# The retention branch's SiLU gate formed where its projection leaves PSUM, and multiplied onto each retention block

## The chip, the cores and the metric

One core of one Trainium2 chip runs the whole program. The metric is the device time of one execution in microseconds. A few names are used throughout: PE is the tensor engine (matmuls, with weight loads listed as PEld), DVE the vector engine, ACT the scalar engine, POOL the engine called GpSimd, and SP the engine whose queue issues every DMA of this kernel. SBUF is the working memory of 128 partitions; PSUM holds what PE writes, in eight banks of 128 x 512 float32 values. Each engine works its own queue in order and waits on semaphores for the others.

## The reference, cut to what matters

One layer is applied to 2048 frames of a new stream and to 64 frames of a running one. A combined projection of 1024 to 6144 columns feeds a differential attention (branch A), a multi-scale retention (branch B), a SiLU gate for each branch (za, zb) and two sigmoid merge gates.

```python
h = rmsnorm(x, norm_g) @ w_in
qa, ka, va, za, qb, kb, vb, zb, ga, gb = jnp.split(h, _split_points(), axis=-1)
...
oa = diff_attention(...)          # 4 heads, 128-d values
ob = retention(...)               # 4 heads, blocks with a carried state
...
oa = (rmsnorm(oa, subln_g) * (1.0 - lam_init)).reshape(B, T, W_A) * jax.nn.silu(za)
ob = rmsnorm(ob).reshape(B, T, W_B) * jax.nn.silu(zb)
m = ga * (oa @ w_oa) + gb * (ob @ w_ob)
return x + m @ w_out
```

The change concerns the line for `ob`: where silu(zb) is formed, and where it is multiplied.

## The kernel before

Matrices are split into a high and a low part (`hi`, `lo`, suffixes `h` and `l`), and three float32r matmuls stand for one product. The frames are worked in two halves of 1024; the 64 sample frames go with the first.

The instruction order is not written out. Each piece of work is a Python generator; a loop runs them by priority over modelled clocks (`self.pe`, `self.act`, `self.dve`, `self.pool`, moved by `P`, `A`, `V`, `G`, with `ld` and `st` for DMAs). A generator yields a modelled time, or a condition, at which it may go on. The order in which generators emit is the order in each engine's queue, and the hardware then runs these fixed queues with its real durations. `take` and `give` count the buffers of a tag (`BUFS`): `mm` 2, `s` 2, `at` 2, `pv` 1 and `tp` 1 are PSUM banks; `ev` 3 and `tlo` 2 are eviction tiles; `row` 10 are the large working rows; `oz` 11, `og` 16 and `ob` 8 serve the output stage.

Three streams run beside one another. `w_stream` (lowest priority) walks through the projection's column blocks of 256: keys, queries and values of the attention first, then vb, qb, kb, then a mark "ret", then za, zb, ga, gb. For a gate it calls `transposed`: `mm_group` (L533, matmuls at L554) fills an `mm` bank with 128 output channels of 512, 320 or 256 frames, and `fin_t` (L853) evicts it: one DVE multiply by the row's RMS factor (L865) into an `ev` tile, the bank given back, and a store to a DRAM scratch tensor (`zaT`, `zbT`, `gaT`, `gbT`). `z_stream` does attention and retention: `qk_block` writes scores to `s` banks (L1052, L1053), DVE evicts them with the distance bias (L1061), softmax runs on ACT and DVE, and `at_pv` transposes and multiplies by the values. The retention blocks (`ret_block`, L1463, 17 of them) follow after the half's attention, and in half 1 partly between heads; each ends with a transpose (L1563), an ACT copy to `res` and four stores to `obT`.

When `z_stream` is done, `out_prep` (L1634) loads, for each group of 264 frames and each branch, four tiles `on` (from `oaT` or `obT`) and four tiles `z`; `og_fin` (L1661) applies SiLU to `z` on ACT (L1664), multiplies on POOL (L1667) and splits the product (ACT cast to `ogh` L1677, DVE subtraction to `ogl` L1680). `out_stream` consumes them in `m_tile` (L1722 to L1724, eight tiles a group, branch A into an `mm` bank, branch B into an `s` bank). The products have buffers for three sets of four, so the set for a group's branch can be cast only when the set three before has had its last matmul. Beside it `gates` loads the merge gates (`gt`, tanh at L1698), `m_fin` combines on DVE (L1742) and POOL (L1746), and `b_prep` prepares the last projection's weights (`wst`, casts to `bh` and `bht` at L1815). The last projection (L1934) closes the program.

Of the kernel before, what the change touches and what calls it, by code (L numbers as in the profile page):

```python
# [11 lines left out]
AF = mybir.ActivationFunctionType  # L12
# [14 lines left out]
GW = 264  # L27
# [9 lines left out]
LAT = 250.0  # L37
# [22 lines left out]
class Hybrid:  # L60
# [771 lines left out]

        return fin

    def transposed(self, half, dst, d0, scale=None, grouped=True, final=False):
        us = []
        groups = [(0, 0, 512), (1, 0, 256), (1, 256, 320)] if half == 0 else [(0, 0, 512), (1, 0, 512)]
        for ct in range(2):
            for k, (seg, col, n) in enumerate(groups):
                yield from self.take("mm")  # L840
                ps = self.psum("mm")[:, :n]
                last = ct == 1 and k == len(groups) - 1
                yield from self.mm_group(ps, n, us, slice(128 * ct, 128 * ct + 128),
                                         (seg, slice(col, col + n)), True, last)
                t0 = 1024 * half + 512 * seg + col
                self.live["t"] += 1
                self.spawn(self.fin_t(ps, n, dst[d0 + ct], t0, scale, grouped, self.pe + LAT), 0, "w")
# [5 lines left out]
    def fin_t(self, ps, n, dst, t0, scale, grouped, t):  # L853
        nc = self.nc
        c0 = t0 % 1024
        last = 8 if n % 128 else (c0 + n) // 128 - 1
        yield lambda: self.tb[last] is not None
        yield from self.take("ev")
        ev = self.sb(self.ep, [128, 512], "ev")[:, :n]
        t = max(t, self.tb[last])  # L860
        if t > self.pe:
            yield t
        rsb = self.rsb[:, c0:c0 + n]
        if scale is None:
            nc.vector.tensor_mul(ev, ps, rsb)  # L865
# [597 lines left out]
    def ret_block(self, k, t0, r, first):  # L1463
        nc = self.nc
        z0 = 0 if r == 128 else 4
# [7 lines left out]
        qt, kt, qx = v3(qk, 0), v3(qk, 1), v3(vx, 1)  # L1473
# [3 lines left out]
        t = self.ld(vb, self.vbN[t0:t0 + r, :], 1 << 18)  # L1477
# [18 lines left out]
        ts = self.V(4 * r, t)  # L1496
# [18 lines left out]
        ru = self.row("rru")  # L1515
# [3 lines left out]
        for h in range(4):  # L1519
            oh = op[:, 128 * h:128 * h + 128]  # L1520
            nc.tensor.matmul(oh, sm[:, h, :], vb[:, 128 * h:128 * h + 128], start=True, stop=first)  # L1521
            to = self.P(512)
            if not first:
                nc.tensor.matmul(oh, qx[:, h, :], state[:, 128 * h:128 * h + 128], start=False, stop=True)
                to = self.P(512)
        if tu > self.pe:
            yield tu
        new = self.sb(self.tp_, [128, 512], "state")
        if first:
            nc.vector.tensor_copy(new, up)  # L1530
            t = self.V(512, tu)
        else:
            for h in range(4):
# [3 lines left out]
                t = self.V(128, tu)  # L1537
# [16 lines left out]
        t = self.V(80)  # L1554
# [23 lines left out]
        self.give("row", self.pe, 2)  # L1578
        self.give("row", t)

    def ret_some(self, b0, n):
# [52 lines left out]
    def out_prep(self):  # L1634
        pa = self.z3p
        self.wo = [[([[self.sb(self.zq, [128, 512], "wa", "woq", F32R) for n in "hl"],
                      [pa.tile([128, 512], F32R, tag=f"wo{n}{br}{kt}", name=f"wo{n}{br}{kt}") for n in "hl"]], {})
                    for kt in range(4)] for br in range(2)]
        for br in range(2):
            yield from self.load_wo(br, 0)  # L1640
        for g in range(8):
            gsl = slice(GW * g, GW * g + GW)
            for br, (oT, zT) in enumerate(((self.oaT, self.zaT), (self.obT, self.zbT))):
                for kt in range(4):
                    yield from self.take("oz", 2)
                    on = self.sb(pa, [128, GW], "oz", "on")
                    z = self.sb(pa, [128, GW], "oz", "z")
                    self.ld(z, zT[kt][:, gsl], 1 << 17)
                    t = self.ld(on, oT[kt][:, gsl], 1 << 17)
                    og = []  # L1650
                    self.ogs.append(og)
                    self.spawn(self.og_fin(on, z, t, og, (2 * g + br) % 3 == 2), 1)
                    yield self.pe
            if g == 0:
                self.spawn(self.gates(), 0)
                for q in range(1, 4):
                    for br in range(2):
                        yield from self.load_wo(br, q)
                yield lambda: self.b_left < 13

    def og_fin(self, on, z, t, og, third):  # L1661
        nc = self.nc
        yield t
        nc.scalar.activation(z, z, AF.Silu)  # L1664
        t = self.A(GW, self.pe)
        yield t
        nc.gpsimd.tensor_mul(on, on, z)  # L1667
        t = self.G(GW, t)
        self.give("oz", t)
# [7 lines left out]
        nc.scalar.copy(h, on)  # L1677
        t = self.A(GW, t)
        yield t
        nc.vector.tensor_sub(l, on, h.bitcast(F32))  # L1680
        t = self.V(GW + 80, t)
        self.give("oz", t)
        og.append((h, l, t))
# [388 lines left out]
    def w_stream(self):  # L2072
# [18 lines left out]
                seq.append((base + 256 * g, lambda half, dst=dst, g=g, sc=sc:  # L2091
                            self.transposed(half, dst, 2 * g, sc, False)))
        seq.append((None, "ret"))
        for base, dst, n in ((za, self.zaT, 2), (zb, self.zbT, 2), (ga, self.gaT, 4), (gb, self.gbT, 4)):
            for g in range(n):
                fin = base == gb and g == n - 1
                seq.append((base + 256 * g, lambda half, dst=dst, g=g, fin=fin:
                            self.transposed(half, dst, 2 * g, final=fin)))
# [76 lines left out]
    def run(self):  # L2175
# [21 lines left out]
        for k in ("ac", "u", "xt", "ob"):  # L2197
            self.res[k].free = []
        self.q_end = self.smx = None
        self.y_at, self.yr = -1, []  # L2200
        self.yq = [{} for _ in range(8)]
        ET = mybir.EngineType
# [93 lines left out]
```

## Time and profile before

| | |
|---|---|
| time, three runs | 1944.99, 1946.57 (median), 1947.22 us |
| the profiled execution | 1945.82 us, span 1944.0 us, mean granted PE clock 0.998 |
| instructions in the span | 33842 |
| DMA | 301 MB in 371904 packets, 52.6% of 16 engines' span |

Below are the page's rows by slices. Each digit is the busy share of one fortieth of the span (48.6 us) in tenths; PEclk is the clock that PE was granted.

```profile
PE   9999999999999999999999999999999999999999
DVE  6753777646666336648856757845773376545643
ACT  7443766544434235535765646544563445653321
POOL 4310112112122121211121111112113356543422
```

PE is nearly full in every slice. DVE varies most: it is high where attention and projection run beside one another, and low at 600 to 720 us and around 1520 us. The output stage (from about 1575 us) is the one place where POOL and ACT rise together. The first gate block is evicted at 385 us, and its places in both halves lie in stretches in which DVE also serves attention. In rows of the views, "idle before" is the time for which an engine sat waiting, with what ended the wait.

### The profile page before, as it was taken

To read this page: it belongs to the slowest core of one execution; us is meant where nothing else is said; L and a number is where in the kernel's file an instruction comes from. 1 tells how busy PE (TensorE), PEld (TensorE's weight loads), DVE (VectorE), ACT (ScalarE), POOL (GpSimd) and SP (SyncE) were. 2 spreads that over 40 slices of the span, in tenths; PEclk is the share of its full clock that TensorE was granted. 3 is DMA by queue.
4 is the path that set the end of the run, shared out by engine and by line. 5 is a ranking of instruction groups with operands and counts; after the bars stand their busy time and mean duration, and the time that the engine had idled before them with its cause. 6 is when DMAs were issued, how large, how long until landed. Compare 5 with 4: busy or idle time off the path is not lost.

```text
span 1944.0 us, 33842 instructions
## 1 busy us (share of the span) xinstructions
PE 1927.5 (99%) x11984; PEld 1731.2 (89%) x11984; DVE 1166.6 (60%) x2798; ACT 964.9 (50%) x2072; POOL 490.1 (25%) x429
## 2 busy tenths in 40 slices
PE   9999999999999999999999999999999999999999
PEld 8779999999988899999998888888888889998887
DVE  6753777646666336648856757845773376545643
ACT  7443766544434235535765646544563445653321
POOL 4310112112122121211121111112113356543422
PEclk9999999999999999999999999999999999999999
DMA  7747454335566655654344253363133678866651
GB/s 235 240 151 199 143 143 132 106 102 156 163 192 187 166 148 168 202 183 141 112 120 128 76 146 96 99 185 116 63 99 108 190 229 259 264 196 189 190 151 65
DMA packets 372074, 303.32 MB, mean 156 GB/s; under 512 B 77440, under 2 KB 334720, under 8 KB 371904
## 3 DMA queue, kind: packets, MB, share of 16 engines
q1 hardware_dynamic: 371904, 301.16, 52.6%
q8 instruction: 94, 1.54, 0.4%
q14 instruction: 76, 0.62, 0.1%
HBM read 195.87 MB, written 100.14 MB: 152 GB/s over the span
## 4 chain that ended last, share of the span: by engine, by line
PE 88%; DVE 5%; DMA 3%; POOL 1%; issue 1%; ACT 1%; SPq 1%; DVEq 0%; POOLq 0%; ACTq 0%
PE mm L554 51%; PE mm L1934 4%; PE s L1052 3%; PE s L1053 3%; PE at L1160 3%; PE at L1934 2%; PE pv L1139 2%; PE pv L1140 2%; PE pv L1138 2%; PE s L1934 1%; PE s L1723 1%; PE s L1724 1%; PE pv L1521 1%; PE mm L1723 1%; PE s L1722 1%
## 5 line engine op out<-in xcount | busy, mean ns | idle before, releaser
L514 POOL TENSOR_TENSOR wl<-ws,wh 128x512 fp32r<-128x512 f32 x191 | 261.4, 1380 | 896.2 <-ACT wh L504 544.9
L554 PE MATMUL mm<-xh,wh 128*128 128x512 f32 (+2 forms) x1280 | 460.7, 360 | 0.0
L554 PE MATMUL mm<-xh,wl 128*128 128x512 f32 (+2 forms) x1280 | 452.7, 354 | 0.0
L554 PE MATMUL mm<-xl,wh 128*128 128x512 f32 (+2 forms) x1280 | 451.9, 353 | 0.0
L554 PEld LDWEIGHTS mm<-xh,wl 128*128 128x128 f32 x1280 | 241.0, 188 | 31.7
L554 PEld LDWEIGHTS mm<-xh,wh 128*128 128x128 f32 x1280 | 241.4, 189 | 29.1 <-issue 0.2
L554 PEld LDWEIGHTS mm<-xl,wh 128*128 128x128 f32 x1280 | 241.6, 189 | 27.8
L554 PE MATMUL mm<-wh,xh 128*128 128x256 f32 (+1 forms) x768 | 236.7, 308 | 0.0
L554 PE MATMUL mm<-wh,xl 128*128 128x256 f32 (+1 forms) x768 | 231.3, 301 | 0.0
L554 PE MATMUL mm<-wl,xh 128*128 128x256 f32 (+1 forms) x768 | 231.0, 301 | 0.0
L1175 DVE TENSOR_TENSOR atl<-at,ath 128x512 fp32r<-128x512 f32 (+1 forms) x144 | 93.7, 659 | 136.2 <-ACT ath L1173 136.1
L504 ACT CAST wh<-ws 128x512 fp32r<-128x512 f32 x192 | 117.0, 617 | 112.6 <-PE mm L554 90.3
L1091 ACT ACTIVATE row<-row,a_mx 128x1024 f32<-128x1024 f32 (+7 forms) x160 | 153.7, 962 | 24.5 <-DVE a_mx L1071 24.3
L554 PEld LDWEIGHTS mm<-wh,xh 128*128 128x128 f32 x768 | 146.3, 190 | 7.1 <-issue 0.5
L554 PEld LDWEIGHTS mm<-wl,xh 128*128 128x128 f32 x768 | 146.4, 191 | 6.7 <-issue 0.5
L554 PEld LDWEIGHTS mm<-wh,xl 128*128 128x128 f32 x768 | 146.3, 190 | 5.5
L865 DVE TENSOR_TENSOR ev<-mm,rsb 128x512 f32<-128x512 f32 x140 | 83.0, 593 | 112.8 <-PE mm L554 112.4
L1173 ACT CAST ath<-at 128x512 fp32r<-128x512 f32 (+1 forms) x144 | 78.7, 563 | 141.5 <-PE at L1160 138.4
L1061 DVE CUSTOM_DVE_ANT_0 row<-s,dfar 128x512 f32<-128x512 f32 (+2 forms) x192 | 118.2, 630 | 46.4 <-PE s L1053 45.9
L1052 PE MATMUL s<-K,q 128*128 128x512 f32 (+3 forms) x320 | 118.4, 374 | 0.7 <-DVE a_acc L1061 0.7
L1053 PE MATMUL s<-K,q 128*128 128x512 f32 (+3 forms) x320 | 115.2, 362 | 0.0
L1110 ACT ACTIVATE row<-row,a_w 128x1024 f32<-128x1024 f32 (+4 forms) x96 | 85.1, 898 | 34.4 <-DVE a_w L1105 31.2
(342 smaller groups left out, 4193.5 us busy)
## 6 DMA issues: line engine op xcount, KB each, us to landing
ws<-in_w_in_dram SPq DMA_DIRECT2D x192, 256.0 KB, 3.1
q<-qT SPq DMA_DIRECT2D x128, 128.0 KB, 3.0
V<-vN SPq DMA_DIRECT2D x24, 512.0 KB, 5.4
K<-kT SPq DMA_DIRECT2D x48, 256.0 KB, 4.3
a<-mT SPq DMA_DIRECT2D x34, 256.0 KB, 4.1
gt<-gaT SPq DMA_DIRECT2D x64, 132.0 KB, 3.2
gt<-gbT SPq DMA_DIRECT2D x64, 132.0 KB, 3.1
mT<-gt SPq DMA_DIRECT2D x64, 132.0 KB, 3.0
```

What stands on the lines that cost most here:

```text
L504: self.nc.scalar.copy(h, st)
L514: self.nc.gpsimd.tensor_sub(l, st, h.bitcast(F32))
L554: nc.tensor.matmul(ps, p, q, start=c == 0 and i == 0, stop=c == KC - 1 and i == 2)
L865: nc.vector.tensor_mul(ev, ps, rsb)
L1052: nc.tensor.matmul(ps, q1s, kk, start=True, stop=False)
L1053: nc.tensor.matmul(ps, q2s, kk, start=False, stop=True)
L1061: nc.vector.tensor_tensor_reduce(out=units[k0 // 1024][:, k0 % 1024:k0 % 1024 + n], in0=ps, in1=tab, scale=-SLOPES[h], scalar=3.0e38, op0= ...
L1091: nc.scalar.activation(u, u, AF.Exp, bias=mx, scale=-1.0, accum_out=lp[:, k:k + 1])
L1110: nc.scalar.activation(u1, u1, AF.Identity, scale=w[:, 1:2])
L1173: nc.scalar.copy(ah[:, :w], at[:, :w])
L1175: nc.vector.tensor_sub(al[:, :w], at[:, :w], ah[:, :w].bitcast(F32))
L1934: nc.tensor.matmul(q[b], u, v, start=fresh and c == 0 and m == 0, stop=c == 3 and m == 2, skip_group_check=True)
```

## The change

Four things are changed.

1. `w_stream` projects zb before za (they change places), in both halves.
2. The eviction of zb forms the whole SiLU: after the multiply on DVE, the `mm` bank is given back as before; then exp(-v) on ACT into a `tlo` tile `ez`, plus 1 and a reciprocal on DVE in place, and the product on POOL back into the `ev` tile, which is stored to `zbT`. A counter `zgate` counts the stores issued in each half.
3. A retention block waits (in the emission order) until all zb stores of its half are issued. After the block's transpose, `ret_out` loads the block's piece of silu(zb) into the free half of its row, multiplies on POOL and then stores to `obT`. `ret_out` is counted in the zone of `z_stream`, which must be empty before `out_prep` starts.
4. In the output stage branch B loads only `on`, and takes one `oz` buffer where it took two; its SiLU on ACT and its multiply on POOL are gone. Branch A is as before.

```diff
     def fin_t(self, ps, n, dst, t0, scale, grouped, silu, t):
...
         t = self.V(n, t)
         self.live["t"] -= 1
         self.give("mm", t)
+        if silu:
+            yield from self.take("tlo")
+            e = self.sb(self.ep, [128, 512], "tlo", "ez")[:, :n]
+            if t > self.pe:
+                yield t
+            nc.scalar.activation(e, ev, AF.Exp, scale=-1.0)
+            t = self.A(n, t)
+            yield t
+            nc.vector.tensor_scalar_add(e, e, 1.0)
+            nc.vector.reciprocal(e, e)
+            self.V(n, t)
+            t = self.V(n)
+            yield t
+            nc.gpsimd.tensor_mul(ev, ev, e)
+            t = self.G(n, t)
+            self.give("tlo", t)
         yield t
         self.give("ev", self.put(dst, ev, t0, n, grouped))
+        if silu:
+            self.zgate[t0 // 1024] += 1
...
# ret_block, ahead of the state's update
+        half = t0 // 1024 if r == 128 else 0
+        yield lambda: self.zgate[half] == 12 - 4 * half
...
         nc.scalar.copy(res, tp)
-        t = self.A(4 * r, t)
-        self.give("tp", t)
+        ts = self.A(4 * r, t)
+        self.give("tp", ts)
+        self.spawn(self.ret_out(ru, t0, r, t, ts), 1, "z")
+        self.give("row", self.pe, 2)
+
+    def ret_out(self, ru, t0, r, t, ts):
+        nc = self.nc
+        yield t
+        zs, res = ru[:, 0:4 * r], ru[:, 512:512 + 4 * r]
+        z3 = zs.rearrange("p (h t) -> p h t", h=4)
+        if r == 128:
+            z0 = GW * (t0 // 256) + t0 % 256
+            tz = self.ld(z3, self.zbT[:, :, z0:z0 + 128].rearrange("h p t -> p h t"), 1 << 18)
+        else:
...
+        yield max(ts, tz)
+        nc.gpsimd.tensor_mul(res, res, zs)
+        t = self.G(4 * r, self.pe)
         yield t
...
# out_prep
-            for br, (oT, zT) in enumerate(((self.oaT, self.zaT), (self.obT, self.zbT))):
+            for br, oT in enumerate((self.oaT, self.obT)):
                 for kt in range(4):
-                    yield from self.take("oz", 2)
+                    yield from self.take("oz", 2 - br)
                     on = self.sb(pa, [128, GW], "oz", "on")
-                    z = self.sb(pa, [128, GW], "oz", "z")
-                    self.ld(z, zT[kt][:, gsl], 1 << 17)
+                    z = None
+                    if br == 0:
+                        z = self.sb(pa, [128, GW], "oz", "z")
+                        self.ld(z, self.zaT[kt][:, gsl], 1 << 17)
...
# og_fin
+        t = self.pe
+        if z is not None:
+            nc.scalar.activation(z, z, AF.Silu)
+            t = self.A(GW, t)
+            yield t
+            nc.gpsimd.tensor_mul(on, on, z)
+            t = self.G(GW, t)
+            self.give("oz", t)
...
# w_stream
-        for base, dst, n in ((za, self.zaT, 2), (zb, self.zbT, 2), (ga, self.gaT, 4), (gb, self.gbT, 4)):
+        for base, dst, n in ((zb, self.zbT, 2), (za, self.zaT, 2), (ga, self.gaT, 4), (gb, self.gbT, 4)):
...
+                            self.transposed(half, dst, 2 * g, final=fin, silu=silu)))
```

In the changed kernel all line numbers behind L871 are larger (L1061 becomes L1079, L1113 becomes L1131, L1664 becomes L1705).

The rows below show DVE's queue in half 1, at the eviction of the fourth group of the gate that stands behind kb. First before, where that gate is za (`ISA` with `row,a_acc<-s` is the eviction of a score bank):

```order
L1071 TENSOR_REDUCE a_mx_14446<-a_acc_14380 128x1
L1061 ISA row_14448,a_acc_14450<-s_14460,dfar_1669 128x512
L1061 ISA a_acc_14450 128x1
L865 TENSOR_TENSOR ev_14459<-mm_14381,rsb_8971 128x512
L930 SCALAR_TENSOR_TENSOR r_sq_14363<-tp_14413,r_sq_14363 128x256
L933 TENSOR_SCALAR r_sq_14363<-r_sq_14363 128x256
L1061 ISA row_14448,a_acc_14450<-s_14469,dfar_1669 128x512
L1061 ISA a_acc_14450 128x1
```

Now, where it is zb, the rows from that group's reciprocal to the next evictions:

```order
L879 TENSOR_SCALAR ez_14559<-ez_14559 128x512
L880 RECIPROCAL ez_14559<-ez_14559 128x512
L961 SCALAR_TENSOR_TENSOR r_o_14479<-r_o_14479,gsub_466,r_y_14481 128x256
L865 TENSOR_TENSOR ev_14629<-mm_14550,rsb_9195 128x512
L1131 SCALAR_TENSOR_TENSOR row_14337<-row_14337,a_w_14588,row_14393 128x1024
L1131 SCALAR_TENSOR_TENSOR row_14338<-row_14338,a_w_14588,row_14394 128x512
L879 TENSOR_SCALAR ez_14640<-ez_14640 128x512
L880 RECIPROCAL ez_14640<-ez_14640 128x512
```

Two rows of 512 columns are added for each group, and the next bank's eviction (L865) and the softmax's combination (now L1131) stand behind them in the same queue.

The second place is ACT's queue in the output stage, ahead of the casts of the products for group 2's branch B (`on` from `obT`), which PE needs right behind its second group. Before:

```order
L1664 ACTIVATE z_18978<-z_18978 128x264
L1815 CAST bht2_18301<-wst_18880 128x512
L1815 CAST bht1_18299<-wst_18879 128x512
L1698 ACTIVATE gt_19008<-gt_19008,bg_464 128x264
L1698 ACTIVATE gt_19009<-gt_19009,bg_464 128x264
L1815 CAST bht3_18303<-wst_18737 128x512
L1677 CAST ogh_19074<-on_18705 128x264
```

Now:

```order
L1705 ACTIVATE z_18988<-z_18988 128x264
L1856 CAST bht2_18422<-wst_18915 128x512
L1739 ACTIVATE gt_19027<-gt_19027,bg_464 128x264
L1739 ACTIVATE gt_19028<-gt_19028,bg_464 128x264
L1856 CAST bht1_18420<-wst_18914 128x512
L1856 CAST bht3_18424<-wst_18802 128x512
L1739 ACTIVATE gt_19064<-gt_19064,bg_464 128x264
L1739 ACTIVATE gt_19065<-gt_19065,bg_464 128x264
L1856 CAST bht4_18426<-wst_18806 128x512
L1739 ACTIVATE gt_19106<-gt_19106,bg_464 128x264
L1739 ACTIVATE gt_19107<-gt_19107,bg_464 128x264
L1718 CAST ogh_19176<-on_18729 128x264
```

Between the last gate tile `z` and the casts stand five more rows than before (four tanh of merge gates and one more cast); the load of that `z` stands two output tiles earlier in SP's queue.

More of the change, by code (lines that the diff above doesn't have):

```diff
@@ L833, in fin_vb, with transposed @@
         return fin
-    def transposed(self, half, dst, d0, scale=None, grouped=True, final=False):
+    def transposed(self, half, dst, d0, scale=None, grouped=True, final=False, silu=False):
         us = []
@@ L846, in transposed @@
                 self.live["t"] += 1
-                self.spawn(self.fin_t(ps, n, dst[d0 + ct], t0, scale, grouped, self.pe + LAT), 0, "w")
+                self.spawn(self.fin_t(ps, n, dst[d0 + ct], t0, scale, grouped, silu, self.pe + LAT), 0, "w")
                 if final and ct == 1 and (k == 0 or last):
@@ L851, in transposed, with fin_t @@
                 yield self.pe
-    def fin_t(self, ps, n, dst, t0, scale, grouped, t):
+    def fin_t(self, ps, n, dst, t0, scale, grouped, silu, t):
         nc = self.nc
@@ L1566, in ret_block @@
         nc.scalar.copy(res, tp)
-        t = self.A(4 * r, t)
-        self.give("tp", t)
+        ts = self.A(4 * r, t)
[11 more added lines that the diff above has]
+        else:
+            for h in range(4):
+                tz = self.ld(z3[:, h].rearrange("p (g c) -> p g c", c=8),
+                             self.zbT[h].rearrange("p (g c) -> p g c", c=GW)[:, :, 256:GW], 1 << 15)
+        yield max(ts, tz)
+        nc.gpsimd.tensor_mul(res, res, zs)
+        t = self.G(4 * r, self.pe)
         yield t
@@ L1577, in ret_block @@
                 t = self.st(d3[:, :, 256:GW], rh.rearrange("p (g c) -> p g c", c=8), 1 << 17)
-        self.give("row", self.pe, 2)
         self.give("row", t)
@@ L1663, in og_fin @@
         yield t
[L1664 to L1669, printed above, removed]
+        t = self.pe
[6 more added lines that the diff above has]
+            self.give("oz", t)
         tag = "ob" if third else "og"
@@ L2093, in w_stream @@
         seq.append((None, "ret"))
-        for base, dst, n in ((za, self.zaT, 2), (zb, self.zbT, 2), (ga, self.gaT, 4), (gb, self.gbT, 4)):
+        for base, dst, n in ((zb, self.zbT, 2), (za, self.zaT, 2), (ga, self.gaT, 4), (gb, self.gbT, 4)):
             for g in range(n):
                 fin = base == gb and g == n - 1
-                seq.append((base + 256 * g, lambda half, dst=dst, g=g, fin=fin:
-                            self.transposed(half, dst, 2 * g, final=fin)))
+                seq.append((base + 256 * g, lambda half, dst=dst, g=g, fin=fin, silu=base == zb:
+                            self.transposed(half, dst, 2 * g, final=fin, silu=silu)))
         seqs = [f + seq for f in first]
@@ L2199, in run @@
         self.q_end = self.smx = None
+        self.zgate = [0, 0]
         self.y_at, self.yr = -1, []
```

## The prediction

> **What bounds the kernel now.** I read the page's busy line and the list of waits first, then the tensor engine (PE) by stage, then the vector engine (DVE) in the two stretches that get new work.
>
> ```profile
> PE 1927.5 (99%) x11984; PEld 1731.2 (89%) x11984; DVE 1166.6 (60%) x2798; ACT 964.9 (50%) x2072; POOL 490.1 (25%) x429
> ...
> PE s L1723 <- DVE ogl L1680: 3.0, 6, 1.7
> PE s L1722 <- ACT ogh L1677: 1.1, 1, 1.1
> ...
> 1590.65 0.29 PE L1723 MATMUL mm<-ogl,woh 128*128 128x264 f32 x1
> 1590.78 0.28 PE L1724 MATMUL mm<-ogh,wol 128*128 128x264 f32 x1
> 1590.90 0.28 PE L1722 MATMUL mm<-ogh,woh 128*128 128x264 f32 x1
> ```
>
> The program is bound by PE from end to end, and PE does the same matmuls after the change. So time can come only from PE's waits, and can go only into new ones. The three matmul rows warn that the 99% flatters: each is shown 0.28 us long, but they start 0.12 us apart, so a short wait can hide inside a row that still reads busy. The two wait rows carry the largest waits, and both lie in the output stage. These rows of busy time by stage (length, then PE, weight load, DVE, ACT, POOL, granted clock, DMA share, GB/s) show it whole, and its worst place:
>
> ```profile
> 1575.00:1765.00 190.00, 185.07 (x1472) 182.69 (x1471) 112.68 (x221) 108.08 (x259) 101.09 (x116) 0.98 0.77 228
> 1620.00:1625.00 5.00, 4.97 (x41) 4.76 (x40) 1.56 (x3) 3.15 (x8) 2.31 (x3) 1.00 0.77 241
> 1625.00:1630.00 5.00, 2.25 (x9) 2.05 (x10) 5.00 (x10) 5.00 (x15) 2.23 (x3) 0.73 0.83 243
> 1630.00:1635.00 5.00, 5.00 (x28) 5.00 (x27) 2.77 (x8) 2.82 (x8) 1.84 (x2) 0.58 0.78 238
> ...
> 1622.90 0.42 ACT L1664 ACTIVATE z<-z 128x264 f32<-128x264 f32 x1 [1.32 <-DMA z<-zaT]
> 1623.23 1.12 ACT L1815 CAST bht<-wst 128x512 fp32r<-128x512 f32 x2
> 1624.26 0.92 ACT L1698 ACTIVATE gt<-gt,bg 128x264 f32<-128x264 f32 x2
> 1625.08 0.60 ACT L1815 CAST bht<-wst 128x512 fp32r<-128x512 f32 x1
> 1625.59 0.72 ACT L1677 CAST ogh<-on 128x264 fp32r<-128x264 f32 x2
> ```
>
> From 1625 to 1630 PE idles 2.75 us, and the granted clock falls to 0.73 and then 0.58. That is 2.75 + 0.27 x 5 + 0.42 x 5 = 6.2 us lost at one place. ACT is the cause: it reached the `ogh` casts only at 1625.59, after a gate z whose load came at 1622.9, the b casts and two tanh.
>
> **The change part by part.** *Output stage.* Gone are 32 loads of z, 32 SiLUs on ACT and 32 multiplies on POOL; the other 32 of each and the one table load stay.
>
> ```profile
> L1664 ACT ACTIVATE z<-z 128x264 f32<-128x264 f32 x64 | 26.8, 421 | 30.7 <-DMA z<-zbT 15.0 <-DMA z<-zaT 14.9 <-POOL gt L1746 0.5
> L1667 POOL TENSOR_TENSOR on<-on,z 128x264 f32<-128x264 f32 x64 | 55.3, 873 | 31.7 <-ACT z L1664 20.2 <-DMA on<-obT 5.0 <-DMA on<-oaT 4.0
> L135 SPq DMA_DIRECT2D z<-zbT x32: 320/382/667, 1539.7 to 1730.8; - x32
> ```
>
> That is 32 x 0.421 = 13.5 us of ACT, 32 x 0.873 = 27.9 us of POOL and 32 x 0.382 = 12.2 us of SP's queue, none of them the bound. They count only through the wait above: by the order the loads ahead of that boundary now stand some two output tiles earlier in SP's queue, since a retention product takes one `oz` buffer and not two. I credit the 6.2 us in full. The other five waits for `ogl`, 3.0 - 1.7 = 1.3 us together, come from the three sets of `og` buffers, which nothing changes. The first loads of the stage come about one projection group (5.4 us) later, since the last retention blocks have a load and a multiply more before the zone closes; ACT has a 13.6 us gap before 1581.1 there (next row), so I cost that at nothing. Without that cover it would be at most 5.4 us.
>
> ```profile
> 1581.10 0.62 ACT L1815 CAST bh<-wst 128x512 fp32r<-128x512 f32 x1 [13.60 <-DMA wst<-in_w_out_dram]
> ```
>
> *Retention blocks.* The wait for the gate's stores costs nothing: in both halves all zb stores stand ahead of the first obT store in SP's order, because zb now goes before za. The extra multiply is 16 x 1.3 us of POOL (L1481 is the nearest row), and the store behind it leaves later; the outputs are read much later, except those of the last four blocks, read in groups 6 and 7.
>
> ```profile
> L1481 POOL TENSOR_TENSOR rvx<-rqk,rtab 128x512 f32<-128x512 f32 x15 | 19.7, 1314 | 33.0 <-DVE a_mx L1071 13.6 <-DMA rqk<-qbT 11.2 <-DMA rvx<-vbN 8.2
> L385 ACT ACTIVATE xroot<-xroot 128x512 f32<-128x512 f32 x4 | 2.5, 632 | 0.1
> ```
>
> *The SiLU at the eviction.* Each of the 20 zb groups (4 x 512, 256 and 320 columns in half 0, 8 x 512 in half 1) gets an exp on ACT (0.63 us for 512, about 11 us in all), an add and a **reciprocal on DVE**, and a POOL multiply (about 24 us at the 1.3 us row). ACT and POOL have room for it. The PSUM bank is handed back before all this, so nothing waits for the new chain itself; but DVE runs in order, and behind each reciprocal stand the score evictions (L1061) and the next projection eviction (L865), for whose banks (two `s`, two `mm`) PE waits.
>
> ```profile
> L395 DVE TENSOR_SCALAR xroot<-xroot 128x512 f32<-128x512 f32 x4 | 2.7, 676 | 0.1
> L933 DVE TENSOR_SCALAR r_sq<-r_sq 128x256 f32<-128x256 f32 x33 | 10.9, 332 | 1.1
> L1103 DVE RECIPROCAL a_w<-a_ls 128x1 f32<-128x1 f32 x64 | 10.5, 164 | 2.2
> L1103 DVE RECIPROCAL a_w<-a_lp 128x1 f32<-128x1 f32 x64 | 7.1, 149 | 0.5 <-ACT row L1091 0.5
> L1236 DVE TENSOR_SCALAR s_acc<-s_acc 128x1 f32<-128x1 f32 x28 | 4.3, 154 | 1.0
> L1274 DVE TENSOR_SCALAR s_mx<-s_mx 128x1 f32<-128x1 f32 x28 | 2.1, 145 | 0.1
> ```
>
> The add is L395 and L933: 0.68 and 0.33 us, and some 0.42 for 320. No row shows a wide reciprocal; the only rows of that instruction hold one element. Lower bound: it streams like L395, 0.68 us for 512. Upper bound: the slowest one-element reciprocal is 164 - 145 = 19 ns above the quickest one-element TENSOR_SCALAR; if all of that is paid per element, it is 0.68 + 512 x 0.019 = 10.4 us. Between these I take the rows at face value: the mean of the two reciprocals, 156.5 ns, less that of the two TENSOR_SCALARs, 149.5, is 7 ns an element above L395's 1.3. That gives 512 x 8.3 ns = **4.3 us** for 512, 2.7 for 320 and 2.1 for 256, called an estimate: it rests on a few nanoseconds, and single rows overlap (149 against 154).
>
> [...]
>
> Now the stretches. za and zb change places, with their weight loads and stores; by its stores za has 380 to 445 us and 1175 to 1250 us before, so zb comes there.
>
> ```profile
> 385.55 0.37 SPq L140 DMA_DIRECT2D zaT<-ev  x1
> 442.56 0.99 SPq L140 DMA_DIRECT2D zaT<-ev  x2
> ...
> 1179.62 18.16 SPq L140 DMA_DIRECT2D zaT<-ev  x3
> 1247.13 0.37 SPq L140 DMA_DIRECT2D zaT<-ev  x1
> ...
> 380.00:445.00 65.00, 65.00 (x423) 60.16 (x422) 36.04 (x89) 29.74 (x61) 14.34 (x13) 1.00 0.37 107
> 1175.00:1250.00 75.00, 74.28 (x391) 63.26 (x390) 57.36 (x153) 47.33 (x92) 11.73 (x10) 1.00 0.27 81
> 900.00:950.00 50.00, 49.28 (x390) 47.94 (x389) 44.33 (x114) 34.34 (x73) 11.02 (x9) 1.00 0.38 122
> ```
>
> Half 0: DVE's 36.0 us, plus reciprocals 4 x (4.3 + 2.1 + 2.7) = 36.4, plus adds 4 x 1.43 = 5.7, is 78 us of work in 65. Half 1: 57.4 + 8 x 4.3 (34.4) + 8 x 0.68 (5.4) = 97 us in 75. PE can run ahead by its two banks only, so DVE becomes the bound: at least 13 + 22 = 35 us, if DVE never waited. The busiest 50 us now have DVE at 0.89, with 0.7 us of PE idle. I take it as filled to 0.92: 78 / 0.92 = 85 and 97 / 0.92 = 105, so +20 and +30 = **+50 us**. At 0.85 it is 92 and 114, +66; half-clock spells like the one at 1630 could add a few us more.
>
> The sum: 1945.8 (the profiled execution; span 1944.0 and 1.8 around it) + 50 - 6 = 1990. The median of the three runs is 1946.6, 0.8 above it, which leaves 1990.
>
> **The rivals.** *Fast reciprocal, the wait removed (faster).* At 0.68 us half 1 holds 57.4 + 2 x 5.4 = 68 us of DVE in 75 and half 0 47 in 65, under or near the 0.92; then only the output stage changes: 1946.6 - 6.2 = 1940. For it speaks that a one-element reciprocal is hardly dearer than its neighbours (149 against 154 ns). It decides in half 1: DVE fills to 0.92 once a 512 reciprocal costs (69 - 57.4 - 5.4) / 8 = 0.8 us, and wholly at 1.5 us. *Fast, and given back:* with DVE at 0.91 in half 1 a few waits of some tenths appear in front of score evictions, and the casts at the boundary stay late because the new ACT order has a b cast and four tanh more ahead of them; about 6 us return and it is 1946. *Between:* a reciprocal of about 2.2 us for 512 puts 57.4 + 17.6 + 5.4 = 80 us into the 75 and 36 + 19 + 6 = 61 into the 65; at 0.92 that is +12 and +1, so 1946.6 + 13 - 6 = 1953. *The change does not do what it says:* the order shows the rows there, so I give this nothing.
>
> **How the numbers follow.** Slow reciprocal, 1965 to 2015: 0.70. Between, 1950 to 1965: 0.07. Fast and given back, 1943 to 1950: 0.11. Fast with the gain: 0.12. About 0.2% (3.9 us) is what a measurement of this kernel tells from no change, so faster 0.12, same 0.11, slower 0.77. The range 1942 to 2015 leaves out most of the fast gain and the tail above 2015, about 0.18; the slow case's own range is 1965 to 2015, from the 35 us floor less the gain to the loose fill with half clock.
>
> **What would show it.** A DVE RECIPROCAL group of 128x512, 12 times: near 4.3 us for me, 0.7 for the rival. In the stretches of zb DVE should be near full, and PE should wait on L1061's and L865's successors; elsewhere, and in za's new places, nothing should change. Around the second boundary of the output stage PE should have no 2.75 us gap and a clock of 1.00. I am wrong if the reciprocal is under 1.5 us, or if PE finds enough work during each reciprocal that neither stretch grows.

## The result and the profile after

| | before | after |
|---|---|---|
| median of the runs, us | 1946.37 (1944.99 to 1947.22, 4 runs) | 1970.71 (1969.04 to 1972.64, 4 runs) |
| after / before | | 1.0126, 95% interval 1.0109 to 1.0144 |
| span of the profiled execution, us | 1944.0 | 1969.6 |

The change makes the kernel 24 us slower. The forecast had the direction, and the time lies in its range of 1942 to 2015; that range also holds "no change", so this alone says little. Its centre, 1990, is 19 us too high. (VectorE is DVE in the rows, ScalarE is ACT, TensorE is PE.)

The answer to the disputed price stands in the groups of VectorE's instructions after, with shapes kept apart (line, operation, out<-in, count, then busy us and mean ns of one, then idle time before):

```profile
L880 DVE RECIPROCAL ez<-ez 128x512 f32<-128x512 f32 x12 | 40.2, 3353 | 0.4
L880 DVE RECIPROCAL ez<-ez 128x320 f32<-128x320 f32 x4 | 8.6, 2153 | 0.1
L880 DVE RECIPROCAL ez<-ez 128x256 f32<-128x256 f32 x4 | 7.0, 1753 | 0.1
```

A reciprocal of 512 columns takes 3.35 us, not 4.3 and not 0.7. Together the twenty take 55.8 us.

Where the time went is read from the busy time in windows at the same times: first before, then after (window, its length, then busy us and instructions of PE, PEld, DVE, ACT and POOL, the granted clock, the DMA share and GB/s).

```profile
380.00:460.00 80.00, 80.00 (x513) 73.79 (x512) 46.50 (x123) 40.02 (x87) 15.37 (x14) 1.00 0.43 123
1175.00:1275.00 100.00, 99.28 (x531) 85.03 (x530) 76.03 (x197) 62.35 (x117) 12.56 (x12) 1.00 0.41 114
...
700.00:750.00 50.00, 50.00 (x333) 46.40 (x332) 20.65 (x50) 16.59 (x35) 7.62 (x6) 1.00 0.56 168
...
1600.00:1650.00 50.00, 47.04 (x359) 46.41 (x358) 36.02 (x66) 29.34 (x71) 31.07 (x33) 0.93 0.84 257
1650.00:1700.00 50.00, 49.15 (x397) 48.37 (x395) 26.52 (x59) 30.63 (x74) 28.45 (x35) 1.00 0.89 263
```

```profile
380.00:460.00 80.00, 73.41 (x463) 66.36 (x463) 74.63 (x120) 37.81 (x77) 26.41 (x25) 1.00 0.33 96
1175.00:1275.00 100.00, 91.73 (x440) 76.43 (x439) 88.08 (x189) 55.29 (x108) 27.37 (x22) 0.95 0.24 74
...
700.00:750.00 50.00, 47.22 (x305) 43.24 (x304) 23.56 (x51) 18.06 (x43) 14.78 (x12) 0.97 0.61 166
...
1600.00:1650.00 50.00, 49.48 (x392) 48.44 (x392) 37.77 (x65) 25.77 (x60) 25.67 (x27) 1.00 0.77 237
1650.00:1700.00 50.00, 46.45 (x355) 45.37 (x354) 28.52 (x61) 25.11 (x60) 20.49 (x23) 0.93 0.79 234
```

Three things are to be seen. In the two stretches of zb, VectorE goes from 46.5 to 74.6 us of 80 and from 76.0 to 88.1 of 100, and PE, which had gaps of 0.0 and 0.7 us there, has 6.6 and 8.3 us of them and does 50 and 91 fewer matmuls in the same time. At 700 to 750 us a loss appears that the prediction did not have. And in the output stage the loss at 1600 to 1650 is gone, but 1650 to 1700 has it now, with the same clock of 0.93. The stage also begins 27.6 us later now (its first matmul is at 1602.5 us, before at 1574.9). Counted from there, PE's waits stand at 51 to 53 us before and at 74 to 78 us after, so the loss went one group of some 24 us further.

The waits of PE after (line, what it waited for: us in all, times, longest):

```profile
PE pv L1158 <- DVE atl L1193: 4.5, 4, 2.9
PE tp L935 <- DVE r_lo L929: 3.6, 4, 1.7
PE s L1070 <- DVE a_acc L1079: 3.4, 2, 2.4
PE mm L554 <- DVE ev L865: 2.4, 2, 1.8
PE tp L418 <- DVE xacc L314: 2.3, 1, 2.3
```

The first four are VectorE's, with 13.2 of their 13.9 us in the zb stretches, and the longest of each of the four ends at a row that stands close behind a reciprocal in VectorE's queue; the fifth is the new loss near 725 us. The longest of all, in order of time, on VectorE and then on PE (start, us, instruction, in brackets the idle time before and what ended it):

```profile
1238.75 0.42 DVE L879 TENSOR_SCALAR ez<-ez 128x512 f32<-128x512 f32 x1
1239.20 3.35 DVE L880 RECIPROCAL ez<-ez 128x512 f32<-128x512 f32 x1
...
1243.90 0.68 DVE L1193 TENSOR_TENSOR atl<-at,ath 128x512 fp32r<-128x512 f32 x1
```

```profile
1241.48 0.28 PE L1157 MATMUL pv<-ath,V 128*128 128x256 f32 x1
1244.63 0.58 PE L1158 MATMUL pv<-atl,V 128*128 128x256 f32 x1 [2.87 <-DVE atl L1193]
```

The reciprocal holds VectorE from 1239.2 to 1242.5. Behind it stand five small softmax rows (0.1 to 0.9 us) and then the low part `atl` that PE's next product needs; PE has ended the product before at 1241.8 and stands for 2.9 us. The next window shows what follows:

```profile
1240.00:1245.00 5.00, 2.13 (x10) 1.65 (x9) 4.89 (x8) 0.93 (x1) 1.28 (x1) 0.87 0.02 7
1245.00:1250.00 5.00, 5.00 (x23) 4.81 (x23) 4.54 (x9) 2.56 (x5) 0.00 (x0) 0.50 0.15 49
```

After the gap the granted clock is 0.50 for these 5 us: PE reads busy throughout, but its matmuls of 256 columns start 0.21 us apart at 1245.2, where at 1241.4 they start 0.12 apart, so more is lost here than the wait's 2.9 us.

### The profile page after: what moved, and what is told of

Read it like the earlier page. It is cut to its first block, busy times and chain, and to the rows that moved or that the text cites. A ratio compares the mean times of both kernels' runs of the same rounds, so it can differ in the third digit from the quotient of the medians.

```text
span 1969.6 us, 33916 instructions
## 1 busy us (share of the span) xinstructions
PE 1935.2 (98%) x11984; PEld 1734.8 (88%) x11984; DVE 1237.1 (63%) x2838; ACT 966.3 (49%) x2060; POOL 510.2 (26%) x434
## 4 chain that ended last, share of the span: by engine, by line
PE 64%; DVE 7%; DMA 3%; issue 2%; ACT 1%; POOL 1%; SPq 1%; POOLq 0%; DVEq 0%; ACTq 0%
PE mm L554 34%; PE mm L1975 4%; PE s L1071 2%; PE s L1070 2%; PE at L1975 2%; PE at L1178 2%; PE pv L1158 1%; PE pv L1157 1%; PE pv L1156 1%; DVE ez L880 1%; PE s L1764 1%; PE s L1975 1%; PE s L1765 1%; PE s L1763 1%; PE mm L1763 1%
## 5 line engine op out<-in xcount | busy, mean ns | idle before, releaser
L865 DVE TENSOR_TENSOR ev<-mm,rsb 128x512 f32<-128x512 f32 x140 | 82.8, 592 | 102.9 <-PE mm L554 100.1
L1079 DVE CUSTOM_DVE_ANT_0 row<-s,dfar 128x512 f32<-128x512 f32 (+2 forms) x192 | 118.2, 629 | 44.6 <-PE s L1071 44.4
L1131 DVE SCALAR_TENSOR_TENSOR row<-row,a_w 128x1024 f32<-128x1024 f32 (+4 forms) x96 | 102.3, 1075 | 4.3 <-ACT row L1128 4.1
```

The costliest lines, as they stand in the source:

```text
L1079: nc.vector.tensor_tensor_reduce(out=units[k0 // 1024][:, k0 % 1024:k0 % 1024 + n], in0=ps, in1=tab, scale=-SLOPES[h], scalar=3.0e38, op0= ...
L1131: nc.vector.scalar_tensor_tensor(out=u0, in0=u0, scalar=w[:, 0:1], in1=u1, op0=ALU.mult, op1=ALU.add)
```

## The experiments

Theory A: VectorE, in order, is held by the reciprocals, and PE waits for the evictions behind them. Rival B: the new order (zb first, gate loads and multiplies in the retention blocks) costs the time. Each run has its own measurements of the kernel before beside it on the same chip; ratios are to those. The first five keep the order of the change on all engines.

**The reciprocal made cheap.**

```diff
-            nc.vector.reciprocal(e, e)
+            nc.vector.tensor_scalar_mul(e, e, 1.0)
```

> The reciprocal of the SiLU is replaced by a multiply by one on the same engine, at the same place; the order of all engines stays that of the change (the gate then holds v(1+exp(-v)) in place of v/(1+exp(-v))). Theory A (VectorE is held by the reciprocal, and TensorE waits for the evictions queued behind it): the loss of the change's trace at 400 to 500 us (9.8 us more than before) and at 1200 to 1300 us (13.8 us more) goes, 1970.7 - 23.6 = about 1947. Rival B (the time is lost by the new order of loads, stores and retention blocks): 1969 to 1972, nothing changes. Both: the waits near 725 us and at the second group boundary of the output stage (1674 us less some 24) stay, since no reciprocal is near them.

Measured: 1946.04 us, ratio 1.001 (1.0001 to 1.002). Its windows:

```profile
380.00:460.00 80.00, 80.00 (x513) 73.33 (x512) 58.68 (x142) 42.76 (x91) 26.52 (x25) 1.00 0.41 120
1175.00:1275.00 100.00, 99.53 (x531) 85.28 (x530) 79.20 (x208) 63.56 (x120) 25.96 (x19) 1.00 0.35 102
```

PE does 513 and 531 matmuls in them, as many as before. PE's order is the same in this run and in the change, so the starts of their matmuls can be compared one by one: the profiled change falls 9.5 us behind over zb's groups in half 0 and 14.4 us behind over those in half 1, and outside of them some 3 us, most of it at the wait for `xacc`. The cheap instruction itself takes 10.5 us for all twenty (783 ns for 256 columns and 574 for 320, means that hold a few long ones):

```profile
L880 DVE TENSOR_SCALAR ez<-ez 128x512 f32<-128x512 f32 x12 | 5.1, 427 | 0.4
```

By the ratios, 0.0126 - 0.0010, so 23 us of the 24, are the reciprocals'; B's share is some 2 us (the interval goes from 0.2 to 4). The two waits without a reciprocal near them stay, as both theories had it: 1.9 us for `xacc`, and 2.3 us for a product cast in the output stage.

**Half of each reciprocal, and two of them.**

```diff
-            nc.vector.reciprocal(e, e)
+            nc.vector.reciprocal(e[:, :n // 2], e[:, :n // 2])
```

> The reciprocal covers only the first half of each tile's columns, so some 1.75 us in place of 3.35 for 512 (the gate's other half keeps 1+exp(-v)); the order stays. Theory A, by the fill: half 1 has 57.4 + 8 x 1.75 + 8 x 0.46 = 75.1 us of VectorE work, 82 us at a fill of 0.92 where 75 are there, so 7 us; half 0 has 36.0 + 15.4 + 7 = 58 us in 65, so nothing: 1947 + 7 = 1954. Rival A2 (each reciprocal's length is paid as it is, in proportion): the middle between the run without it and the change, 1959. Rival B: 1969 to 1972.

```diff
             nc.vector.reciprocal(e, e)
+            nc.vector.reciprocal(e, e)
```

> The reciprocal is issued twice in a row, 6.7 us for 512 (the gate then holds v(1+exp(-v))); the order stays. Theory A: VectorE is already full in both stretches, so every added us comes on top: 1970.7 + 55.8 = 2026, up to 2032 with half-clock spells. Rival A2 (in proportion, 24 us for the first set): 1970.7 + 24 = 1995. Rival B: 1971.

Measured: 1947.18 us with halves (ratio 1.0009, 1.0 to 1.0018) and 2031.98 with two (1.0444, 1.0429 to 1.046). The cost is no proportion. Over the run with the cheap instruction (which itself takes 10.5 us), the first 29 us of reciprocals (21.0 + 4.6 + 3.8) cost nothing that the ratios can tell apart (1.0009 against 1.001), the next 26 cost some 23, and the 56 after those some 62, more than themselves. That is a queue that fills up. With the halves the windows show VectorE just below that point, and PE almost without loss:

```profile
380.00:460.00 80.00, 79.87 (x511) 73.31 (x510) 66.13 (x142) 43.08 (x90) 26.54 (x25) 1.00 0.41 121
1175.00:1275.00 100.00, 99.17 (x528) 84.50 (x527) 87.49 (x208) 62.94 (x117) 25.65 (x19) 1.00 0.33 98
```

With two, the waits of the change are all there and larger; the two largest (the lines stand one further):

```profile
PE pv L1159 <- DVE atl L1194: 14.3, 5, 4.7
PE mm L554 <- DVE ev L865: 12.1, 5, 5.1
```

My sum for the halves had been 7 us; it used the narrow stretches of the prediction, one of the steps that failed (below).

**Every second one, at full length.** The sum of VectorE's work is that of the halves, the length of one block that of the change.

```diff
-            nc.vector.reciprocal(e, e)
+            self.nz += 1; (nc.vector.reciprocal(e, e) if self.nz % 2 else nc.vector.tensor_scalar_mul(e, e, 1.0))
```

> The change with the reciprocal in every second group only, at its full length (3.35 us for 512), the others with the multiply by one; the order stays. VectorE's sum is within 0.5 us of that of the run with half reciprocals everywhere, the length of a block is that of the change. Theory A1 (the sum of VectorE's work in the stretch decides): 54.8 + 14.5 = 69 us in 80 and 75.8 + 13.4 = 89 in 100, under a fill of 0.92, so as with the halves: 1946 to 1949. Theory A2 (the length of a block decides): half of the change's loss, 1946 + 12 = 1958.

Measured: 1952.6 us, ratio 1.004 (1.0026 to 1.0054), so between the two theories: some 5 us more than with the halves, and 5 less than half of the change's loss would give. One wait, again behind a reciprocal, makes a good part of it:

```profile
PE s L1070 <- DVE a_acc L1079: 2.5, 2, 2.4
```

Both count: the sum sets the bulk, and a block of 3.35 us adds some us by where it falls.

**The gate on ScalarE.**

```diff
-            nc.vector.tensor_scalar_add(e, e, 1.0)
-            nc.vector.reciprocal(e, e)
+            nc.scalar.activation(e, e, AF.Ln, bias=1.0)
+            nc.scalar.activation(e, e, AF.Exp, scale=-1.0)
```

> The same gate without VectorE: the add and the reciprocal become ln(1 + e) and exp(-that) on ScalarE, at the same place in the order and with the planner told nothing of it. Theory A: as with the cheap operation, 1947, plus what 2 x 0.63 us on ScalarE per group of 512 cost: its share of busy time in these stretches is some 0.5, so 0 to 3 us, 1947 to 1950. Rival B: 1969 to 1972. Rival A3 (what counts is how long the gate's chain takes, on whatever engine): near 1971 too, with waits on ScalarE.

Measured: 1945.96 us, ratio 1.0006 (0.9997 to 1.0015): no difference from before. One pass of 512 columns takes 0.63 us, and in the stretches PE has no gap:

```profile
380.00:460.00 80.00, 80.00 (x511) 73.42 (x510) 46.45 (x118) 53.76 (x114) 26.16 (x25) 1.00 0.41 121
1175.00:1275.00 100.00, 100.00 (x536) 86.02 (x535) 74.52 (x202) 71.38 (x133) 26.56 (x20) 1.00 0.34 102
```

ScalarE goes to 0.67 and 0.71 busy and can hold it; VectorE is back at before's 46.5 and below its 76.0. So nothing is left of the loss once VectorE is spared, and A3's 1971 did not come. A3 itself is not tested by this, since two passes, 1.3 us, are also shorter than one reciprocal, and a long chain on another engine was not tried. Against it speak the change's own four largest waits: they end at rows of VectorE behind a reciprocal, not at a row of the gate's chain.

**Cut in pieces.**

```diff
-            nc.vector.reciprocal(e, e)
-            self.V(n, t)
-            t = self.V(n)
+            t = self.V(n, t)
+            for c in range(0, n, 128):
+                ec = e[:, c:min(n, c + 128)]
+                yield t
+                nc.vector.reciprocal(ec, ec)
+                t = self.V(768, t)
```

> The change with each reciprocal cut into pieces of 128 columns (about 0.95 us each by the rate of the change's trace, 63 us in all in place of 56), each a step of its own, so that other VectorE work comes in between; the planner counts their true length. Theory A1 (what counts is how much VectorE has to do in the stretch): no better than the change, 1965 to 1980. Theory A2 (what counts is how long one instruction holds the queue, since TensorE runs ahead by its banks only): near the run without the reciprocal, 1946 to 1952.

Measured: 1973.15 us, ratio 1.0147 (1.0131 to 1.0163), as A1 had it. But the order is the planner's own here. PE's longest wait (first row) is for an eviction that stands in VectorE's queue behind pieces and rows of other work, and the slower chain holds its `ev` tiles longer, so that VectorE itself waits for the store of one (second row):

```profile
467.61 0.63 PE L554 MATMUL mm<-xh,wh 128*128 128x320 f32 x1 [5.67 <-DVE ev L865]
...
469.60 0.42 DVE L865 TENSOR_TENSOR ev<-mm,rsb 128x256 f32<-128x256 f32 x1 [1.19 <-DMA zbT<-ev]
```

So it shows that pieces are no cure in this form, and not by itself that length is nothing; the run with every second reciprocal is the cleaner one.

**The planner told the price, and the ScalarE form told too.**

```diff
-            t = self.V(n)
+            t = self.V(6 * n)
```

> The change with the planner counting 3.4 us for a reciprocal of 512 columns in place of 0.7; instructions as in the change, the order is the planner's own. If the loss is that VectorE's evictions are queued behind a block that the planner took for short: half of it or more goes, 1948 to 1960. If the sum of VectorE's work alone decides: 1965 to 1975.

For the other, the two `activation` calls of the ScalarE form are counted with `self.A(n, t)` each, and nothing on VectorE.

> The gate on ScalarE, and the planner counts the two passes of ScalarE and nothing on VectorE; the order is the planner's own. If only the reciprocal cost time: 1944 to 1949, as with the order left alone. If the planner's order is itself worth some us: outside of that.

Measured: 1958.56 us (1.0074, 1.006 to 1.0089) and 1957.99 (1.0069, 1.0055 to 1.0082). The first looks like "half of the loss goes", but the second has no reciprocal at all and is as slow. Its windows tell a part of why:

```profile
1175.00:1275.00 100.00, 100.00 (x525) 85.37 (x524) 69.91 (x199) 71.59 (x136) 27.23 (x22) 1.00 0.29 89
700.00:800.00 100.00, 95.64 (x682) 90.05 (x681) 54.18 (x108) 44.27 (x93) 22.38 (x17) 0.98 0.53 156
1580.00:1700.00 120.00, 112.64 (x846) 109.15 (x845) 76.56 (x153) 63.17 (x150) 52.15 (x58) 0.96 0.77 235
```

The zb stretch is clean; 4.4 and 7.4 us of PE are lost elsewhere, where the planner's new order happens to wait. In the same two windows the ScalarE form at the change's order loses 4.2 and 4.5, so these make 3 us of the difference of 11 between the two profiled executions; where the rest goes was not followed. With the price told, the zb stretches keep 2.4 and 2.6 us of gaps in place of the change's 6.6 and 8.3:

```profile
380.00:460.00 80.00, 77.57 (x493) 70.67 (x492) 77.11 (x126) 37.90 (x76) 27.08 (x25) 1.00 0.37 108
...
1175.00:1275.00 100.00, 97.44 (x489) 82.16 (x488) 89.33 (x178) 51.92 (x101) 27.57 (x23) 1.00 0.28 88
```

So a right price helps where it applies, and the planner's reshuffle of all that follows can be worth as much: the ScalarE form at the kept order and at its own stand at 1.0006 and 1.0069, 12 us apart. What one edit costs is only read at a kept order.

**The output stage alone.** The kernel before, with the output stage's part of the diff and nothing else.

> The kernel before with only the output stage's part of the change: the retention products take one tile and no gate (no z load, SiLU or multiply for them; the retention branch's gate is left out of y altogether), projections and retention blocks as before. My prediction credited this part with 6.2 us: about 1938.5 on this chip (before is at 1944.7 here), and no wait for the casts of the products at any group boundary. Rival C (the output stage's loads come in the same bursts as before, and when the SiLUs go, another boundary has its late transfer): 1943 to 1946, with a wait of 1.5 us or more for those casts, or for the gates, at another boundary.

Measured: 1943.04 us, ratio 0.9994 (0.9985 to 1.0003). Not 6 us: about 1, and the interval holds zero. PE's row of it:

```profile
1651.69 0.39 PE L1726 MATMUL s<-ogh,woq 128*128 128x264 f32 x1 [2.08 <-ACT ogh L1681]
```

A wait of this kind is still there, one group later than before's, whose casts began at 1625.6 us. In the change's order with the gate on ScalarE it stands in ScalarE's rows like this, in order of time:

```profile
1653.90 0.92 ACT L1739 ACTIVATE gt<-gt,bg 128x264 f32<-128x264 f32 x2 [4.11 <-DMA gt<-gaT]
...
1656.50 1.34 ACT L1718 CAST ogh<-on 128x264 fp32r<-128x264 f32 x4
```

The casts that PE needs stand behind a tanh for whose transfer ScalarE waits 4.1 us, and just before it SP's queue has four loads of 256 KB back to back:

```profile
1645.95 1.85 SPq L135 DMA_DIRECT2D wst<-in_w_out_dram  x4
```

**Those loads spread, and the tanh later.** Both on the ScalarE form; PE's order is that of the change throughout, and up to 1550 us the order of the other engines is that of the ScalarE form too.

```diff
             t = self.ld(raw[k], w[128 * r:128 * r + 128, n:n + 512], 1 << 18)
             self.b_left -= 1
+            yield self.pe + 1500
```

> The gate on ScalarE as before, and in the output stage the four loads of 256 KB for the output weight's matrices are planned at least 1.5 us apart, not back to back. Theory C (such a burst delays the gates' transfer, ScalarE waits for it 4.1 us with the product casts queued behind, and TensorE waits for those at 1654 us): that wait and its half clock go, 1946 - 6 = 1940. Rival C2 (the output stage is short of transfers as a whole, its share being 0.8 to 0.9 there, so that another boundary waits in its place): 1944 to 1948.

Measured: 1944.26 us, ratio 0.9998 (0.9988 to 1.0008): the wait at 1654 us is gone, and one of 1.5 us stands at the next boundary, 1675 us, as C2 had it. ScalarE still waits 3.4 us for a transfer of `gt` at 1665 us, so that the burst alone makes them late is not shown. Against the run without it (1.0006, 0.9997 to 1.0015) the intervals overlap, so a gain is not shown. With the second edit on top:

```diff
     def gate(self, n, ct, pair, t):
-        yield t
+        yield t + 2000
```

> The kernel with the gate on ScalarE and the spread loads, and the planner asks for the gates' tanh 2 us later, so that fewer of them stand ahead of the product casts on ScalarE while their transfer is still under way. If ScalarE's order at the group boundaries is what keeps the output stage's 6 us: 1944 - 3 to 5 = 1939 to 1941, no wait over 1 us for a product cast. If the wait goes to yet another boundary, or to the multiply that follows the tanh: 1943 to 1946.

Measured: 1941.88 us, ratio 0.9982 (0.9973 to 0.9991), 0.9 us above the upper end expected and 1.1 below the rival's lower end. The largest wait for a product cast is 1.2 us (in the profiled execution, with 1938.52 us the fastest of the eleven):

```profile
PE s L1763 <- ACT ogh L1718: 1.2, 1, 1.2
```

This is the one version measured as faster than both kernels, by 0.18% over the kernel before; it took the gate off VectorE and a new order of ScalarE at the group boundaries. How much each of the last two edits gives is not told apart.

**The gate loaded earlier in a retention block.** The loss at 700 to 750 us comes with the change's order: from 690 to 740 us PE has 50.0 us busy before, and 47.9, 46.8 and 45.8 with the cheap instruction, with halves and on ScalarE. Its size changes from execution to execution: the two runs with the spread loads have the order of the ScalarE form up to there and 46.9 and 47.3 us. PE waits there for `xacc`, the sum of squares of the second half's x, whose loads need the `row` tiles that the retention blocks use too. The edit loads the gate into the free half of `rqk` right behind the state update:

```diff
         self.ret_at += 1
+        zs = qk[:, 512:512 + 4 * r]
+        z3 = zs.rearrange("p (h t) -> p h t", h=4)
+        if r == 128:
+            zc = GW * (t0 // 256) + t0 % 256
+            tz = self.ld(z3, self.zbT[:, :, zc:zc + 128].rearrange("h p t -> p h t"), 1 << 18)
...
-        self.spawn(self.ret_out(ru, t0, r, t, ts), 1, "z")
-        self.give("row", self.pe, 2)
+        self.spawn(self.ret_out(ru, t0, r, t, ts, zs, tz), 1, "z")
+        self.give("row", self.pe)
```

> The gate formed on ScalarE (ln and exp) with the order as the planner then makes it around one more edit: a retention block loads its gate's columns right after its state update, into the half of its q/k tile that is then free, and not at its end. Theory D (the x loads of the second half come late because retention blocks keep their row tiles during the gate load; that is the wait near 715 us with its half clock, 7 us more at 700 to 800 us than before): the wait goes, 1946 - 6 = 1940. Rival: the wait stays or another one of its size takes its place, 1945 to 1948.

Measured: 1946.07 us, ratio 1.0011 (1.0002 to 1.002). The rival: the wait for `xacc` shrinks to 0.9 us, and one of 2.8 us, at 772 us and for a retention block's output to leave its bank, stands there instead:

```profile
PE tp L418 <- ACT rru L1595: 2.8, 1, 2.8
```

So this loss is in every run with the change's order and not before; which part of the retention blocks' new rows causes it stays open.

## Why the prediction was right, and where it was off

**The mechanism was right.** Wide reciprocals in VectorE's queue, PE waiting for the evictions behind them, in za's old places: all there, and the run with a cheap instruction in its place takes 23 of the 24 us away. The waits named, for the score eviction and the projection eviction, are 5.8 of the 13.9 us of the four largest groups; the other 8.1 are for `atl` and `r_lo`, low parts that stand in the same queue and that the prediction did not name.

**The price of a reciprocal was too high.** The step took 8.3 ns an element from differences of one-element rows; it is 6.25 ns an element and 0.15 us besides (3353 - 1753 = 1600 ns for 256 more columns). That a difference of 7 ns between rows that overlap came so near was luck. With the measured rows the prediction's own sum gives (36.0 + 29.0 + 5.7) / 0.92 = 77 us in 65 and (57.4 + 26.8 + 5.4) / 0.92 = 97 in 75: +34, not +50. This is the larger part of the error, 16 us.

**The stretches were too narrow.** 65 and 75 us came from the stores of za, and the sum let none of VectorE's other work move out of them. Windows of 80 and 100 us around zb's groups take in slack in which VectorE can catch up. From the run with the cheap instruction, less that instruction (8 x 0.43 = 3.4 us in half 1, the other 7.1 in half 0), VectorE has 51.6 us of other work in 80 and 75.8 in 100. The change's windows show it filled to (74.6 + 88.1) / 180 = 0.90. Then the full reciprocals give (51.6 + 29.0) / 0.90 = 90 and (75.8 + 26.8) / 0.90 = 114, +24 against 23 measured; two of them +86 against 84 by the ratios; halves 0 against 0. By halves it holds too: +10 and +14 against 9.5 and 14.4 when the matmuls of the change and of the cheap run are compared one by one, +42 and +44 against 42 and 43 with two. But the widths and the 0.90 were chosen with the change's runs known, so only the other two runs test them. The fill that the prediction took, 0.92, was not the error: between the first and the last reciprocal of each half VectorE is busy 0.94 of the time in the change.

```profile
388.00:460.00 72.00, 65.41 (x408) 58.89 (x408) 67.53 (x100) 33.49 (x69) 25.67 (x24) 1.00 0.34 99
1195.00:1280.00 85.00, 76.73 (x376) 64.11 (x375) 79.80 (x147) 46.33 (x89) 22.54 (x17) 0.94 0.20 63
```

The reckoning misses the run with every second reciprocal, +1 against some 6, where the length of a block shows. By subtraction the narrow stretches were worth 34 - 23 = 11 us.

**The credit of 6.2 us in the output stage failed.** The step was that the wait for the product casts at 1626 us goes when the SiLUs do. It went, but the next boundary has its own late transfer, and the gain of that part alone is 1 us (0.9994) with an interval that holds zero. The prediction had this as a rival ("given back") and did not carry it into the forecast's own sum. The 6.2 was also a little high as a reading: it counts the lower clock over 5 us of which PE stood still for 2.75. By the matmuls of the same three rows (41, then 9 and 28) the loss is 45 matmuls, 5.5 us.

**What was costed at nothing.** The gate's wait for the stores and the extra multiplies show no wait of PE of their own, as said. But the order with the new retention rows has the loss at 700 to 750 us, 2.8 us of PE with a clock of 0.97, which was in no term. With what little the rest gains, all but the reciprocals comes to 1 to 2 us (1.001, and 1.0006 with the gate on ScalarE).

Put together: 1946.4 before, plus 23 for the reciprocals and 1 to 2 for the rest, is 1971 against 1970.7 measured (the 23 is itself measured, so this is a balance and no test). The forecast was 16 us too high by the price and 11 by the stretches, and too low by the 6 that it took off and by the 1 to 2.

**The rivals.** The fast reciprocal is out: 3.35 us against the 0.8 to 1.5 from which it decided. The trace shows it several times slower an element than its neighbours (3353 ns where the multiply by one of the same 512 columns takes 427), but its 6.25 ns are fewer than the 8.3 of the prediction's estimate. The price that the first rival took from the row of another operation, 0.68 us (1.3 ns an element), does not hold for this instruction.

## What to carry to other kernels

Price an operation from a row of its own width; where the trace shows none, keep the range as wide as its two ends: here 0.68 and 10.4 us held the truth, and the point between them made most of the error. In these runs an engine with slack took a dear instruction for next to nothing until its queue was full in that stretch (the first 29 us of reciprocals), and from then on each us came on top (some 23 us for the next 26, some 62 for the 56 after those); long blocks cost some us by where they fell (some 5 with every second reciprocal at full length). So ask for the work per stretch, with the stretch drawn as wide as the work can move. And a wait taken away at one group boundary was worth little here (about 1 us, where 6.2 were credited), since the next one had a late transfer of its own and the same queue.

## What the runs showed of the hardware

The reciprocal on VectorE goes by the element over all widths run here: 952 ns for 128 columns, 1154 for 160, 1753 for 256, 2153 for 320, 3353 for 512, so 6.25 ns each and some 152 ns besides. The first two are the halves' run:

```profile
L880 DVE RECIPROCAL ez<-ez 128x160 f32<-128x160 f32 x4 | 4.6, 1154 | 0.1
L880 DVE RECIPROCAL ez<-ez 128x128 f32<-128x128 f32 x4 | 3.8, 952 | 0.1
```

Ln and Exp of the same 512 columns on ScalarE take 0.63 us each, together well under half of a reciprocal's 3.35 (in order, the two passes):

```profile
L879 ACT ACTIVATE ez<-ez 128x512 f32<-128x512 f32 x12 | 7.5, 627 | 0.2
L880 ACT ACTIVATE ez<-ez 128x512 f32<-128x512 f32 x12 | 7.6, 632 | 0.4
```
